# A rotary-embedding kernel: the first small store carries 512 bytes a partition, and batch 0 then leaves whole

## The chip, the cores and the metric

The kernel runs on one core of a Trainium2 chip. The metric is the device time of one execution in microseconds (us); lower is better. The kernel before takes 316.79 us, the median of three runs that lie between 316.6 and 317.02.

## What is computed

Each row of `x` has 64 values, of which the first 32 and the last 32 are rotated against each other by the cosines and sines of their place in the sequence:

```python
def setup_inputs():
    batch, seq_len, num_heads, head_dim = (8, 2048, 16, 64)
    ...
def reference(x, cos, sin):
    x1 = x[..., :head_dim // 2].copy()
    x2 = x[..., head_dim // 2:].copy()
    cos = cos[None, :, None, :].copy()
    sin = sin[None, :, None, :].copy()
    out1 = x1 * cos - x2 * sin
    out2 = x1 * sin + x2 * cos
    return np.concatenate([out1, out2], axis=-1).astype(np.float32)
```

`x` and the result are float32 in HBM, 8 batches of 2048 by 16 by 64. There is little arithmetic for each byte that is moved: each batch is read once and written once.

## The kernel before

**Tiling.** A batch's 2048 sequence positions are spread over the 128 partitions, J = 16 consecutive positions on each. So a partition holds 16 rows of 16 heads by 64 values: 1024 values a row, which are 4 KB in HBM as float32, and 64 KB a partition and batch, contiguous in HBM. In SBUF the rows are float16 (2 KB a row): the DMAs that GpSimd issues convert while they move. The tile `buf` has five slots (NBUF), and batch b uses slot b % 5, so that batches 5, 6 and 7 go into the slots of 0, 1 and 2 once these have been stored.

**The DMAs and their order.** `load` (L71) and `store` (L81) issue on GpSimd's queue. `in_ring` ties each of these DMAs behind the one issued before, so that the order in the program text is the order on the ring. A DMA that must wait for data holds up all that stand behind it on GpSimd. SyncE's queue carries the float32 tables `sin_f` and `cos_f` and the first JA = 2 rows of batch 0 (`head`), and at the end the last two rows of batch 7.

**The arithmetic.** `rotate(b, j0, j1)` is three VectorE instructions on rows j0 to j1 of a batch: the product with the sines with the halves swapped (L92, into `v`), the product with the cosines in place (L98) and the sum in place (L100). ScalarE converts the tables and the head rows (L104 to L110).

**The order around the change.** Load batch 0 (its 14 rows behind the head) and batch 1. When the head rows and the tables are there, rotate rows 0 and 1 of batch 0 and store row 0 (the small first store, L112): it needs L100 of that small rotation, and the loads of batches 2, 3 and 4 (L113, L114) stand behind it. Then rotate the other 14 rows of batch 0 and store rows 1 to 15 (L116), rotate and store batches 1 and 2, load batches 5 and 6 as one DMA when the slots 0 and 1 have been stored, load 7 when slot 2 has been, and so on to the end.

Of the kernel before, what the change touches and what calls it, by code (L numbers as in the profile page):

```python
# [1 line left out]

# [4 lines left out]


@with_exitstack  # L10
def kernel(
    ctx: ExitStack,
    tc: tile.TileContext,
    x: bass.AP,
    cos: bass.AP,
    sin: bass.AP,
    out: bass.AP,
):
    nc = tc.nc
    f16 = mybir.dt.float16  # L20
    f32 = mybir.dt.float32

    B, S, H, D = x.shape
    Dh = D // 2
    P = nc.NUM_PARTITIONS
    J = S // P
    NBUF = 5

    const_pool = ctx.enter_context(tc.tile_pool(name="rope_const", bufs=1))
    io_pool = ctx.enter_context(tc.tile_pool(name="rope_io", bufs=1))  # L30
    tmp_pool = ctx.enter_context(tc.tile_pool(name="rope_tmp", bufs=1))

    JA = 2
    head = const_pool.tile([P, JA, H, D], f32)
    x0 = x[0].rearrange("(p j) h d -> p j (h d)", j=J)
    sin_f = const_pool.tile([P, J, Dh], f32)
    cos_f = const_pool.tile([P, J, Dh], f32)
    cos_h = const_pool.tile([P, J, Dh], f16)
    sin_h = const_pool.tile([P, J, D], f16)
    nc.sync.dma_start(out=sin_f, in_=sin.rearrange("(p j) d -> p j d", j=J))  # L40
    nc.sync.dma_start(  # L41
        out=head.rearrange("p j h d -> p (j h d)"),
        in_=x0[:, 0:JA, :].rearrange("p j f -> p (j f)"),
    )
    nc.sync.dma_start(out=cos_f, in_=cos.rearrange("(p j) d -> p j d", j=J))

    buf = io_pool.tile([P, NBUF, J, H, D], f16)

    ring = []

    def in_ring(dma):
        if ring:
            tc.add_manual_dep(
                dma.ins,
                ring[-1].ins.name,
                mybir.DependencyInfo(mybir.DependencyClass.NoSync, mybir.DependencyReason.DATA),
                reason="order of the ring",
            )
        ring.append(dma)
        return dma  # L60

    def load(b, n=1):
        k = b % NBUF
        if n == 1:
            j0 = JA if b == 0 else 0
            dst = buf[:, k, j0:J, :, :].rearrange("p j h d -> p (j h d)")
            src = x[b].rearrange("(p j) h d -> p j (h d)", j=J)[:, j0:J, :].rearrange("p j f -> p (j f)")
        else:
            dst = buf[:, k : k + n, :, :, :].rearrange("p b j h d -> p b (j h d)")
            src = x[b : b + n].rearrange("b (p j) h d -> p b (j h d)", j=J)  # L70
        in_ring(nc.gpsimd.dma_start(out=dst, in_=src))  # L71

    def store(b, n=1, j0=0, j1=J):
        k = b % NBUF
        if n == 1:
            src = buf[:, k, j0:j1, :, :].rearrange("p j h d -> p (j h d)")
            dst = out[b].rearrange("(p j) h d -> p j (h d)", j=J)[:, j0:j1, :].rearrange("p j f -> p (j f)")
        else:
            src = buf[:, k : k + n, :, :, :].rearrange("p b j h d -> p b (j h d)")
            dst = out[b : b + n].rearrange("b (p j) h d -> p b (j h d)", j=J)  # L80
        return in_ring(nc.gpsimd.dma_start(out=dst, in_=src))  # L81

    def rotate(b, j0=0, j1=J):
        v = tmp_pool.tile([P, J, H, D], f16)
        n = j1 - j0
        js = slice(j0, j1)
        xt = buf[:, b % NBUF, js, :, :]
        shape = [P, n, H, 2, Dh]
        sin_b = sin_h[:, js, :].rearrange("p j (e d) -> p j e d", e=2).unsqueeze(2).to_broadcast(shape)
        cos_b = cos_h[:, js, :].unsqueeze(2).to_broadcast([P, n, 2 * H, Dh])  # L90
        xe = xt.rearrange("p j h (e d) -> p j h e d", e=2)
        nc.vector.tensor_mul(  # L92
            out=v[:, js, :, :].rearrange("p j h (e d) -> p j h e d", e=2),
            in0=xe[:, :, :, ::-1, :],
            in1=sin_b,
        )
        xw = xt.rearrange("p j h (e d) -> p j (h e) d", d=Dh)
        nc.vector.tensor_mul(out=xw, in0=xw, in1=cos_b)  # L98
        xa = xt.rearrange("p j h d -> p (j h d)")
        nc.vector.tensor_add(out=xa, in0=xa, in1=v[:, js, :, :].rearrange("p j h d -> p (j h d)"))  # L100

    load(0)
    load(1)
    nc.scalar.copy(out=sin_h[:, :, Dh:D], in_=sin_f)  # L104
    nc.scalar.mul(out=sin_h[:, :, 0:Dh], in_=sin_f, mul=-1.0)  # L105
    nc.scalar.copy(  # L106
        out=buf[:, 0, 0:JA, :, :].rearrange("p j h d -> p (j h d)"),
        in_=head.rearrange("p j h d -> p (j h d)"),
    )
    nc.scalar.copy(out=cos_h, in_=cos_f)  # L110
    rotate(0, 0, JA)
    store(0, 1, 0, 1)  # L112
    load(2, 2)  # L113
    load(4)  # L114
    rotate(0, JA, J)
    store(0, 1, 1, J)  # L116
    rotate(1)
    store(1)
    rotate(2)
    store(2)  # L120
    load(5, 2)
    load(7)
    rotate(3)
    rotate(4)
    store(3, 2)
    rotate(5)
    rotate(6)
    store(5, 2)
    rotate(7)
    gate = store(7, 1, 0, 9)  # L130
    store(7, 1, 9, J - JA)
    last = buf[:, 7 % NBUF, J - JA : J, :, :].rearrange("p j h d -> p (j h d)")
    dst = out[B - 1].rearrange("(p j) h d -> p j (h d)", j=J)[:, J - JA : J, :].rearrange("p j f -> p (j f)")
    nc.scalar.copy(out=head.rearrange("p j h d -> p (j h d)"), in_=last)  # L134
    end = nc.sync.dma_start(out=dst, in_=head.rearrange("p j h d -> p (j h d)"))
    tc.add_manual_dep(
        end.ins,
        gate.ins.name,
        mybir.DependencyInfo(mybir.DependencyClass.Sync, mybir.DependencyReason.DATA),
        reason="the last rows go out behind this part",  # L140
    )


# [1 line left out]
_INS = ['x', 'cos', 'sin']  # L145
_OUTS = [((8, 2048, 16, 64), 'float32')]


# [23 lines left out]
```

## Time and profile before

| what | value |
|---|---|
| median of three runs | 316.79 us |
| the profiled execution | 316.6 us, of which the span of instructions is 314.8 us |
| DMAs on GpSimd's queue | 14, of which 8 stores |
| the small first store | 512 KB into HBM, 15.2 us from issue to landing |
| batch 0's second store | 7680 KB into HBM, 68.3 us from issue to landing |
| chain that ended last | 66% VectorE, 13% loads that landed late, 8% the load of `cos_f` |

Time from issue to landing contains the time in which a DMA stands behind others on the ring. KB in that list of DMAs are counted at the destination, so that a batch is 4096 KB where it is loaded and 8192 KB where it is stored. In the same way the GB/s of a slice count bytes as they land: the loads show about half of what the stores show, though both move 64 KB of float32 a partition and batch on the side of HBM:

```profile
GB/s 284 187 262 200 200 266 200 200 262 204 200 200 317 382 492 407 400 400 533 400 200 208 258 200 200 229 237 333 400 491 441 400 400 525 408 400 400 433 427 339
```

Stores of batches 0 to 2 are the slices 13 to 20, those of 3 to 7 the slices from 28 on. Packets are counted in the slice or stretch in which they start, with their whole length and time; on all 16 engines they start at nearly the same moment, so a share can exceed 1 in a short stretch and be 0 in the next.

### The profile page before, as it was taken

How to read it: one execution, taken by the hardware profiler on the slowest of the kernel's cores; microseconds unless marked ns; L12 is line 12 of the kernel's file. 1: busy time of each engine (PE TensorE's matmuls, PEld its weight loads, DVE VectorE, ACT ScalarE, POOL GpSimd, SP SyncE). 2: the span in 40 equal slices, each digit the busy share in tenths (PEclk: the TensorE clock that was granted, in tenths of full speed). 3: DMA queues.
4: the chain of work that ended last, by engine and by line, in shares of the span. 5: the costliest groups of instructions: out<-in, count | busy, mean ns of one | idle time of the engine just before them, and what ended most of it. 6: DMA issues, size and time to landing. Idle time of an engine off the chain costs nothing.

```text
span 314.8 us, 115 instructions
## 1 busy us (share of the span) xinstructions
DVE 209.1 (66%) x27; ACT 6.8 (2%) x6; POOL 8.6 (3%) x18
## 2 busy tenths in 40 slices
DVE  0105999999499999999950000899999999910000
ACT  3200000000000000000000000000000000020000
POOL 1002000000000000000010000000000000010000
DMA  9899999999999899999999999999999999999998
GB/s 284 187 262 200 200 266 200 200 262 204 200 200 317 382 492 407 400 400 533 400 200 208 258 200 200 229 237 333 400 491 441 400 400 525 408 400 400 433 427 339
DMA packets 3104, 101.71 MB, mean 323 GB/s; under 512 B 288, under 2 KB 288, under 8 KB 672
## 3 DMA queue, kind: packets, MB, share of 16 engines
q0 software_dynamic: 2528, 99.09, 98.1%
q1 hardware_dynamic: 576, 2.62, 2.2%
HBM read 67.63 MB, written 67.11 MB: 428 GB/s over the span
## 4 chain that ended last, share of the span: by engine, by line
DVE 66%; another core or an unknown queue 13%; DMA 8%; ACT 1%; issue 0%; SPq 0%; DVEq 0%; ACTq 0%
DVE buf L98 22%; DVE buf L100 22%; DVE v L92 22%; DMA cos_f<-in_cos_dram 8%; ACT head L134 1%; ACT cos_h L110 0%; SPq L41 0%; SPq L40 0%; DVEq L92 0%; ACTq L134 0%
## 5 line engine op out<-in xcount | busy, mean ns | idle before, releaser
L92 DVE TENSOR_TENSOR v<-buf,sin_h 128x16384 f16<-128x16384 f16 (+2 forms) x9 | 69.7, 7744 | 51.4 <-DMA buf<-in_x_dram 41.2
L98 DVE TENSOR_TENSOR buf<-buf,cos_h 128x16384 f16<-128x16384 f16 (+2 forms) x9 | 69.7, 7744 | 15.8 <-ACT cos_h L110 15.5
L100 DVE TENSOR_TENSOR buf<-buf,v 128x16384 f16<-128x16384 f16 (+2 forms) x9 | 69.7, 7744 | 0.3
L81 POOL DMA_DIRECT2D out_dram<-buf x8 | 4.7, 586 | 219.4 <-DVE buf L100 219.4
L134 ACT CAST head<-buf 128x2048 f32<-128x2048 f16 x1 | 1.9, 1898 | 249.9 <-DVE buf L100 249.9
L71 POOL DMA_DIRECT2D buf<-in_x_dram x6 | 3.7, 628 | 49.7 <-DMA out_dram<-buf 48.9
L106 ACT CAST buf<-head 128x2048 f16<-128x2048 f32 x1 | 1.9, 1897 | 3.5 <-DMA head<-in_x_dram 3.5
L104 ACT ACT_TABLE_LOAD x1 | 1.3, 1283 | 0.7 <-PEq L156 0.7
L110 ACT CAST cos_h<-cos_f 128x512 f16<-128x512 f32 x1 | 0.6, 617 | 16.1 <-DMA cos_f<-in_cos_dram 16.1
L104 ACT CAST sin_h<-sin_f 128x512 f16<-128x512 f32 x1 | 0.6, 617 | 1.4 <-DMA sin_f<-in_sin_dram 1.4
L105 ACT ACTIVATE sin_h<-sin_f 128x512 f16<-128x512 f32 x1 | 0.6, 624 | 0.0
L156 POOL MEMSET const-float32-0.0<- 128x1 f32 x1 | 0.1, 100 | 0.2 <-issue 0.2
L156 POOL MEMSET const-bfloat16-1.0<- 128x1 bf16 x1 | 0.1, 103 | 0.0
L156 POOL MEMSET const-float32-1.0<- 128x1 f32 x1 | 0.1, 100 | 0.0
L156 POOL MEMSET const-uint8-127<- 128x1 uint8 x1 | 0.1, 100 | 0.0
## 6 DMA issues: line engine op xcount, KB each, us to landing
buf<-in_x_dram POOLq DMA_DIRECT2D x2, 8192.0 KB, 55.2
buf<-in_x_dram POOLq DMA_DIRECT2D x3, 4096.0 KB, 57.4
out_dram<-buf POOLq DMA_DIRECT2D x1, 7680.0 KB, 68.3
out_dram<-buf POOLq DMA_DIRECT2D x1, 4608.0 KB, 28.6
buf<-in_x_dram POOLq DMA_DIRECT2D x1, 3584.0 KB, 22.3
out_dram<-buf POOLq DMA_DIRECT2D x1, 2560.0 KB, 34.1
head<-in_x_dram SPq DMA_DIRECT2D x1, 1024.0 KB, 6.9
out_dram<-head SPq DMA_DIRECT2D x1, 1024.0 KB, 8.4
```

The lines of the kernel that those rows point to most:

```text
L71: in_ring(nc.gpsimd.dma_start(out=dst, in_=src))
L81: return in_ring(nc.gpsimd.dma_start(out=dst, in_=src))
L92: nc.vector.tensor_mul(out=v[:, js, :, :].rearrange("p j h (e d) -> p j h e d", e=2), in0=xe[:, :, :, ::-1, :], in1=sin_b,)
L98: nc.vector.tensor_mul(out=xw, in0=xw, in1=cos_b)
L100: nc.vector.tensor_add(out=xa, in0=xa, in1=v[:, js, :, :].rearrange("p j h d -> p (j h d)"))
L104: nc.scalar.copy(out=sin_h[:, :, Dh:D], in_=sin_f)
L105: nc.scalar.mul(out=sin_h[:, :, 0:Dh], in_=sin_f, mul=-1.0)
L106: nc.scalar.copy(out=buf[:, 0, 0:JA, :, :].rearrange("p j h d -> p (j h d)"), in_=head.rearrange("p j h d -> p (j h d)"),)
L110: nc.scalar.copy(out=cos_h, in_=cos_f)
L134: nc.scalar.copy(out=head.rearrange("p j h d -> p (j h d)"), in_=last)
L156: nc = _bacc.Bacc("TRN2", target_bir_lowering=False, num_devices=1)
```

## The change

The small first store takes the first two heads of row 0 (128 of 1024 values, 512 bytes of the result on each partition, 64 KB in all) in place of the whole row (4 KB, 512 KB in all). It keeps its place in the ring, between the load of batch 1 and that of batches 2 and 3. The later store of batch 0 carries all 16 rows in place of rows 1 to 15, so that the 512 bytes are written twice, with the same values.

```diff
     rotate(0, 0, JA)
-    store(0, 1, 0, 1)
+    in_ring(
+        nc.gpsimd.dma_start(
+            out=out[0].rearrange("(p j) h d -> p j (h d)", j=J)[:, 0, 0:128],
+            in_=buf[:, 0, 0, 0:2, :].rearrange("p h d -> p (h d)"),
+        )
+    )
     load(2, 2)
     load(4)
     rotate(0, JA, J)
-    store(0, 1, 1, J)
+    store(0)
     rotate(1)
     store(1)
```

## The prediction

> **What bounds the kernel now.** I read the page first, its slices, queues and chain, then the order in time, then short stretches.
>
> ```profile
> span 314.8 us, 115 instructions
> DVE 209.1 (66%) x27; ACT 6.8 (2%) x6; POOL 8.6 (3%) x18
> ...
> DMA  9899999999999899999999999999999999999998
> ...
> q0 software_dynamic: 2528, 99.09, 98.1%
> q1 hardware_dynamic: 576, 2.62, 2.2%
> HBM read 67.63 MB, written 67.11 MB: 428 GB/s over the span
> ```
>
> The DMA engines are busy in every slice and the queue that GpSimd feeds fills 98.1% of 16 engines' span. VectorE, though it owns 66% of the chain of waits, idles 41.2 us for loads. So the time is the sum of the packets on the ring, as long as the ring never runs dry. The order in time says whether it does:
>
> ```profile
> 29.53 0.54 POOL L81 DMA_DIRECT2D out_dram<-buf  x1 [27.08 <-DVE buf L100]
> 30.06 1.26 POOL L71 DMA_DIRECT2D buf<-in_x_dram  x2
> ...
> 52.52 0.54 POOL L81 DMA_DIRECT2D out_dram<-buf  x1 [21.19 <-DVE buf L100]
> ...
> 83.38 8.69 DVE L92 TENSOR_TENSOR v<-buf,sin_h 128x16384 f16<-128x16384 f16 x1 [4.99 <-DMA buf<-in_x_dram]
> ...
> 140.72 0.71 POOL L71 DMA_DIRECT2D buf<-in_x_dram  x1 [30.36 <-DMA out_dram<-buf]
> ...
> 250.69 0.73 POOL L81 DMA_DIRECT2D out_dram<-buf  x1 [87.79 <-DVE buf L100]
> ```
>
> At 29.53 the small store goes onto the ring, at 30.06 the loads of batches 2 to 4, while batch 1's load still runs until about 42.7. Batch 0's second part follows at 52.52, long before its turn at 102. The closest issue is that of batches 5 and 6 at 250.69: the ring's work then ends near 256, a margin of 5 us.
>
> Next, what a packet costs. In the software queue a DMA is one packet a partition and batch, and 16 closing ones: ten DMAs of one batch or less and four of two are 10 by 128 + 4 by 256 + 14 by 16 = 2,528, the queue's count above. So one batch is 8 packets on each of 16 engines. In a short stretch, packets = GB/s by length over packet size, and us of one = DMA share by length by 16 over packets.
>
> ```profile
> core 0: us, DVE busy (x) ACT busy (x) POOL busy (x), PEclk, DMA share, GB/s
> 37.40:38.40 1.00, 1.00 (x1) 0.00 (x0) 0.00 (x0) 1.00 2.43 524
> 39.80:40.80 1.00, 1.00 (x1) 0.00 (x0) 0.00 (x0) 1.00 2.83 524
> 42.60:43.90 1.30, 1.30 (x1) 0.00 (x0) 0.00 (x0) 1.00 1.07 366
> 104.00:105.00 1.00, 1.00 (x1) 0.00 (x0) 0.00 (x0) 1.00 2.30 983
> 144.00:145.00 1.00, 0.96 (x2) 0.00 (x0) 0.00 (x0) 1.00 2.45 1049
> 305.70:309.70 4.00, 0.00 (x0) 0.00 (x0) 0.00 (x0) 1.00 1.05 435
> 1.70:2.00 0.30, 0.00 (x0) 0.30 (x1) 0.30 (x2) 1.00 0.77 130
> 3.00:5.00 2.00, 0.00 (x0) 1.15 (x2) 0.00 (x0) 1.00 0.98 415
> ```
>
> First row: 524 GB/s in 1 us is 16 load packets of 32 KB as they land (64 KB as read), 2.43 us each. Third: 366 by 1.3 is 476 KB, 116 packets of the small store's 4 KB, and 1.07 by 1.3 by 16 over 116 is **0.19 us** each. Fourth: 16 packets of batch 0's remaining 60 KB, **2.30**. Fifth: 16 of a whole batch's 64 KB, **2.45**. Sixth: 85 of the 20 KB store near the end, 0.79. These four store sizes lie on one line: (2.45 - 0.19) / 60 is 0.0377 us a KB, and 0.19 - 4 by 0.0377 leaves 0.04 us for a packet of no length. Second row: the last packet of batch 1's load, just ahead of the small store, takes 2.83, so 0.40 more than its fellows. No such excess stands ahead of the whole-batch stores.
>
> **The change part by part**, each term for one engine, since all 16 carry the same.
>
> 1. The 4 KB store goes: 8 by 0.19 = -1.52 us.
> 2. Batch 0's later store carries 64 KB a partition and not 60: 8 by (2.45 - 2.30) = +1.20.
> 3. A store of 512 bytes a partition comes: no row shows such packets. The line gives 0.04 + 0.5 by 0.0377 = 0.06 us, so 8 by 0.06 = +0.48. Bounds: below, the loads on SP's queue in the last row (415 by 2 over 8.192 is 101 packets of 8 KB, 0.31 each, of which 8 by 0.0377 = 0.30 is length) have only 0.01 fixed, so 0.03 each and 0.24 in all, or nothing if the following load's reads cover them; above, a packet that costs no less than the 4 KB one, 0.19 and 1.52 (the seventh row, 2 KB loads at the start, 19 packets, also gives 0.19). I take the line: same queue, same direction, four sizes. Between the ends it is the store row of 4 KB that is nearest, and the line passes through it.
> 4. The 0.40 us ahead of the small store: kept, since what it is seen at is a short store behind a load, and that stays; if it goes with the bytes, -0.40. Nothing in the rows has it grow.
> 5. Hidden: POOL's issue count stays at 14 and the small store's issue stays at 0.54 us, under batch 1's load (13 us of it left at 29.53; without that cover 0.54). Batch 0's whole store now writes bytes of the output that the small one wrote, so it may have to wait for that to land, with the stores of batches 1 and 2 queued behind it on POOL; but the small packets end by 44.4, and the store waits for VectorE until 52.52, 8 us later. The loads of batches 2 and 3 start and land 1.04 us earlier (1.52 - 0.48), which shortens the 4.99 us idle at 83.38; nothing comes of it, since the stores of batches 1 and 2 stand on the ring behind batch 0's. What is late next: batch 1's store lands 0.16 later, the load at 140.72 as well, under batch 2's store (8 by 2.45 = 19.6 us of cover). The 5 us margin at 250.69 loses nothing, since VectorE's chain from there and the ring's shift together.
>
> The sum: -1.52 + 1.20 + 0.48 = **+0.16 us**, 64 KB more over a ring that is always full. The profiled execution took 316.6 (span 314.8 and 1.8 around it), so 316.8; the median of the runs is 316.79, so **316.9** there.
>
> A rule that speaks against the change stands in the Trainium skill: "DMA: Bandwidth & Descriptors", section Bandwidth, lists a GpSimd DMA of 64 KB over 128 partitions (this store's size) at 0.95 us of DMA time and calls transfers below that size dominated by their descriptors. With that for the 0.48 of step 3, an estimate from this page, the sum would be +0.63. The trace of before has no transfer of that size, and the table is of loads.
>
> **The rivals.** A measurement of this kernel can tell about 0.2%, 0.63 us, from no change.
>
> A, the forecast: the packets lie near the line; -0.3 to +0.6 us, about 316.5 to 317.4. For it: four sizes on one line, and the full ring. Chance 0.50.
>
> B, **slower**: a store packet of 512 bytes has a floor, in place of 0.04 of fixed cost, and load(2, 2) starts that much later on all engines. It decides from (0.63 + 0.32) / 8 = 0.12 us a packet on. At 0.19, the price of the 4 KB one, the sum is -1.52 + 1.20 + 1.52 = +1.20, so 318.0. For it: the 2 KB loads at the start at 0.19, and the 0.40 us that shows a short store to cost more than its bytes. Against: the fit's small intercept, and that the start is cold. The 0.95 us of the Trainium skill's "DMA: Bandwidth & Descriptors", section Bandwidth, would be this case at its beginning. Chance 0.33.
>
> C, **faster**: the row's price was mostly one of turning the engines from reads to writes, and a store that small goes under the loads beside it: terms 3 and 4 become 0 and -0.40, -1.52 + 1.20 - 0.40 = -0.72, so 316.1. For it: the excess of 0.40 at this place alone. Against: the engines work their packets one behind the other, and the whole-batch stores behind loads show no excess. It passes 0.2% only where nearly all of both terms goes. Chance 0.14.
>
> D, the change does nothing of the kind, since what counts is only where POOL stands still until 29.53, which stays; then the bytes alone count, 64 KB at 428 GB/s, +0.15 us, so 316.9. Hardly to be told from A. Chance 0.03.
>
> **How the numbers follow.** The likeliest is A: 316.9. The range reaches down to C's 316.1, with 0.1 of scatter (the three runs span 0.4), and up over B's 318.0 by 0.4, for floors above 0.19 that no row bounds: 316.0 to 318.4. Faster by over 0.2%: C's 0.14. Within: A's 0.50 and D's 0.03, 0.53. Slower: B's 0.33. Below 316.0 and above 318.4 I leave about 0.15.
>
> **What would show it.** Right: a short stretch after 42.7 with packets near 0.06 us; a first VectorE instruction of batch 2 at about 82.3 in place of 83.38; batch 0's store with 64 KB packets at 2.45 and 8 of them in 19.6 us; the load behind batch 1's store issued at about 140.9. B shows as that VectorE instruction at or behind 83.3 and the load at 141.9. C: it comes at 81.5, and the load at 140.0. Wrong altogether: a slice of the span with idle DMA engines, a wait on POOL at 52.5 for the small store, or a packet rate away from this line that differs on whole batches.

## The result and the profile after

The changed kernel takes 317.31 us in the median of 15 runs, the kernel before beside it 316.62: a ratio of 1.0027, with a 95% interval of 1.0017 to 1.0037. It is slower by some 0.7 us. The predicted 316.9 is 0.4 too low, within its range of 316.0 to 318.4; a rise of 0.69 lies just above A's bound of +0.6, and the sign is that of rival B, which had 0.33, but not for B's reason. Medians are of all runs, ratios and intervals leave out the few executions, of this and of other kernels here, that took 5 to 9 us longer.

The page and the order in time of the kernel after (columns of the latter as before: start, length, engine, line, operation):

```profile
span 315.5 us, 115 instructions
...
q0 software_dynamic: 2528, 99.16, 98.1%
```
```profile
52.62 0.54 POOL L81 DMA_DIRECT2D out_dram<-buf  x1 [21.19 <-DVE buf L100]
...
81.97 8.69 DVE L92 TENSOR_TENSOR v<-buf,sin_h 128x16384 f16<-128x16384 f16 x1 [3.47 <-DMA buf<-in_x_dram]
...
141.36 0.71 POOL L71 DMA_DIRECT2D buf<-in_x_dram  x1 [32.42 <-DMA out_dram<-buf]
```

The ring is as full as before, and GpSimd waits at 52.62 for VectorE, not for the small store's landing. Batch 2's first VectorE instruction starts at 81.97, 1.41 us earlier than before, where the forecast had 1.04. And yet the load behind batch 1's store is issued at 141.36, 0.64 later than before, where the forecast had 0.16. So what was lost was lost between 82 and 141, after the small store had done better than expected. Short stretches of the kernel after (length, the three engines, the clock, the DMA share, GB/s; with 16 packets in a stretch of 1 us the share is the time of one packet in us):

```profile
39.70:40.70 1.00, 1.00 (x1) 0.00 (x0) 0.00 (x0) 1.00 2.43 524
42.20:43.00 0.80, 0.80 (x1) 0.00 (x0) 0.00 (x0) 1.00 3.67 737
97.90:98.90 1.00, 1.00 (x1) 0.00 (x0) 0.00 (x0) 1.00 3.40 524
214.70:215.70 1.00, 1.00 (x1) 0.00 (x0) 0.00 (x0) 1.00 2.43 524
```

and the last load packets ahead of the two later turns from loads to stores in the kernel before, which the prediction called free of an excess without a row:

```profile
99.40:100.40 1.00, 1.00 (x1) 0.00 (x0) 0.00 (x0) 1.00 2.43 524
214.10:215.10 1.00, 1.00 (x1) 0.00 (x0) 0.00 (x0) 1.00 2.43 524
```

In the second row of the kernel after, 737 by 0.8 is 590 KB: 16 load packets (524 KB) and 128 of 512 bytes (66 KB). Of 3.67 by 0.8 by 16 = 47.0 us, 16 by 2.43 = 38.9 are the loads'; the rest over 128 is 0.063 us a packet, with the closing packets of two DMAs counted in. As recorded, the price of the short packet was met.

A record, however, is longer than the time that its packet takes up on the ring. A stretch inside the small store of the kernel before shows it:

```profile
43.00:43.90 0.90, 0.90 (x1) 0.00 (x0) 0.00 (x0) 1.00 1.26 432
```

432 by 0.9 is 389 KB, 95 packets of 4 KB, so on each engine one starts every 0.152 us, and each is recorded with 1.26 by 0.9 by 16 over 95 = 0.19 us. The 0.04 us between the two is overlap with the next packet, and it is also what the prediction's line gives a packet of no length. So the 4 KB store and the 512-byte one are each about 8 by 0.04 = 0.3 us shorter on the ring than the sum of their records. In the difference of the two this cancels.

But batch 1's last load packet is no longer late (2.43 for 2.83), and the last packet of **batch 4's load, just ahead of batch 0's store**, is: 3.40, an excess of 0.97 us at a place that had none. The first three of the terms that follow come to -1.42, and batch 2's VectorE instruction came 1.41 earlier. The whole sum is -1.52 + 8 by 0.063 - 0.40 + 1.20 + 0.97 = +0.75, against 0.67 between the two profiled executions (317.27 and 316.6).

### The profile page after: what moved, and what is told of

Same layout as the page of the kernel before. It is cut to its first block, busy times and chain, and to the rows that moved or that the text cites. A ratio compares the mean times of both kernels' runs of the same rounds, so it can differ in the third digit from the quotient of the medians.

```text
span 315.5 us, 115 instructions
## 1 busy us (share of the span) xinstructions
DVE 209.1 (66%) x27; ACT 6.8 (2%) x6; POOL 8.6 (3%) x18
## 4 chain that ended last, share of the span: by engine, by line
DVE 66%; another core or an unknown queue 13%; DMA 8%; ACT 1%; issue 0%; SPq 0%; DVEq 0%; ACTq 0%
DVE buf L98 22%; DVE buf L100 22%; DVE v L92 22%; DMA cos_f<-in_cos_dram 8%; ACT head L139 1%; ACT cos_h L110 0%; SPq L41 0%; SPq L40 0%; DVEq L92 0%; ACTq L139 0%
```

## The experiments

What had to be explained is an excess that stands once in an execution: 0.40 us ahead of a row of 4 KB, 0.97 ahead of a whole batch when 512 bytes went first, and none at any later turn (the rows near 99 and 214). **Theory T**: a cost of the first store that is long enough, paid once. **Rival W**: a cost of writing bytes twice. **Rival A**: a cost of addresses written for the first time. Two more theories came out of the runs. **Theory F**: the loads of batches 0 to 4 together last until about 101.55, whatever short store stands among them, and batch 0's store waits for that. **Theory L**: the engines read ahead of what they write, and the excess is the time of a store's first reads, unless the reads are ahead already. In the stretches below, 2.43 is a load packet on time, and each stretch is from one profiled execution of its kernel.

### No small store at all

```diff
-    in_ring(
-        nc.gpsimd.dma_start(
-            out=out[0].rearrange("(p j) h d -> p j (h d)", j=J)[:, 0, 0:128],
-            in_=buf[:, 0, 0, 0:2, :].rearrange("p h d -> p (h d)"),
-        )
-    )
```

> The changed kernel without its first small store; the loads of batches 2 to 4 are therefore issued at about 2.5 us and not at 30. Theory T: the first store of some length in an execution makes the last load packets ahead of it late, once; a row of 4 KB paid 0.40 us, a whole batch of 64 KB packets pays 0.96, 512 bytes pay nothing and spare nothing. Then the last packets of batch 4's load are long by about 0.96 us as in the changed kernel, and the time is 316.62 - 1.51 - 0.40 + 1.20 + 0.96 = 316.9, some 0.46 below the changed kernel. Rival W: the 0.96 came from bytes that are written twice. Here nothing is, so no excess, and 316.62 - 1.51 - 0.40 + 1.20 = 315.9.

317.28 us against 316.63, ratio 1.0021 (1.0011 to 1.003).

```profile
39.70:40.70 1.00, 1.00 (x1) 0.00 (x0) 0.00 (x0) 1.00 2.43 524
81.10:82.10 1.00, 0.01 (x1) 0.00 (x0) 0.00 (x0) 1.00 2.60 524
98.10:99.10 1.00, 1.00 (x1) 0.00 (x0) 0.00 (x0) 1.00 2.96 524
```

Nothing is written twice, and the excess is there, 0.53 ahead of batch 0's store and the rest in smaller pieces from 52 us on (0.17 at 81): W falls. Summed over the records of all its load packets the excess is some 1.1 us, near the 0.96 that T had, but T's time is 0.4 too low: it took the row's removal as 1.51 us, the sum of its records, where 8 by 0.152 = 1.22 leave the ring. The time is that of the changed kernel. On the ring 512 bytes are worth less than their records, and they spare the next turn little (0.97 is left, of some 1.1).

### A row of 4 KB, written twice, and to another place

Both replace the small store of the changed kernel, whose later store of the whole batch stays:

```diff
+    store(0, 1, 0, 1)
```
```diff
+            out=out[1].rearrange("(p j) h d -> p j (h d)", j=J)[:, 0, 0:1024],
+            in_=buf[:, 0, 0, 0:16, :].rearrange("p h d -> p (h d)"),
```

> The small store is the whole row of 4 KB as before, but batch 0 then leaves whole, so the row is written twice. Theory T: excess of about 0.40 us behind batch 1's load, none ahead of batch 0's store; time 316.62 + 1.20 = 317.8. Rival W (bytes written twice): an excess of about 1 us ahead of batch 0's store as well, time 318.8.

> The small store is a row of 4 KB of batch 0's results, but it goes where batch 1's first row belongs, which batch 1's own store overwrites later; batch 0 leaves whole. Theory T: as in the row written twice, 0.40 us behind batch 1's load and none ahead of batch 0's store, 317.8. Rival A: the cost belongs to addresses of the result that were not written before. Then the excess of about 0.96 us is there ahead of batch 0's store, and the time 318.8.

317.91 (ratio 1.0039, 1.0024 to 1.0054) and 317.88 (1.0042, 1.0027 to 1.0057). First the row written twice, then the row in batch 1's place:

```profile
39.60:40.60 1.00, 1.00 (x1) 0.00 (x0) 0.00 (x0) 1.00 2.79 524
99.20:100.20 1.00, 1.00 (x1) 0.00 (x0) 0.00 (x0) 1.00 2.43 524
```
```profile
39.50:40.50 1.00, 1.00 (x1) 0.00 (x0) 0.00 (x0) 1.00 2.80 524
99.10:100.10 1.00, 1.00 (x1) 0.00 (x0) 0.00 (x0) 1.00 2.43 524
```

Both give the 1.2 us of the extra bytes (1.28 and 1.25) and no excess ahead of batch 0's store. A row spares that store its excess even when its bytes go to other addresses: A falls, and W a second time.

### Half a row, a quarter, and one packet on each engine

The small store of the changed kernel with `0:512` and `0:256` in place of `0:128`; and a row of 16 partitions alone:

```diff
+            out=out[0].rearrange("(p j) h d -> p j (h d)", j=J)[0:16, 0, :],
+            in_=buf[0:16, 0, 0, :, :].rearrange("p h d -> p (h d)"),
```

> The small store carries 2 KB a partition (half a row), batch 0 leaves whole. By the line of store packets 8 by 0.115 = 0.92 us, so 316.62 - 1.51 + 0.92 + 1.20 = 317.2 with the 0.40 us of the row. Theory T leaves open from which size on a first store takes the cost on itself: if 2 KB does, the excess is 0.2 to 0.4 us behind batch 1's load and none later, 317.0 to 317.2; if 2 KB does not, the 0.96 us come ahead of batch 0's store, 317.8.

> The small store carries 1 KB a partition, batch 0 leaves whole. Theory F: batch 0's store again starts at 101.5 to 101.6, 317.3. Theory T: 1 KB either pays off the cost (about 0.1 us of excess behind batch 1's load, none later; start near 101.0, 316.7) or spares nothing (0.96 ahead of batch 0's store, start at 101.8, 317.6).

> The small store is the row of 4 KB, but of 16 partitions alone, one packet on each DMA engine in place of eight; batch 0 leaves whole. Theory T (the first store long enough pays once, a packet of 4 KB is): about 0.2 us for the packet and 0.05 to 0.4 of excess behind batch 1's load, none ahead of batch 0's store, so its first packets start near 100.8 and the time is 316.4 to 316.8. Theory F, formed on the runs without a small store and with half a row, where batch 0's store started at 101.52 and 101.58 on the mean of the engines, as in the changed kernel (101.56): the loads of batches 0 to 4 together need until about 101.55, a short store among them runs beside that, and batch 0's store waits for what is left. Then it starts at 101.55, with 0.8 to 1.0 of excess ahead of it, and the time is that of the changed kernel, 317.3.

317.45 (1.0026, 1.0016 to 1.0036), 317.94 (1.0036, 1.0022 to 1.005, of 5 runs; its profiled one took 317.54) and 317.36 (1.0031, 1.0015 to 1.0047). Half a row, a quarter, one packet on each engine:

```profile
39.60:40.60 1.00, 1.00 (x1) 0.00 (x0) 0.00 (x0) 1.00 2.63 524
98.30:99.30 1.00, 1.00 (x1) 0.00 (x0) 0.00 (x0) 1.00 2.80 524
```
```profile
39.70:40.70 1.00, 1.00 (x1) 0.00 (x0) 0.00 (x0) 1.00 2.58 524
98.30:99.30 1.00, 1.00 (x1) 0.00 (x0) 0.00 (x0) 1.00 3.09 524
```
```profile
39.60:40.60 1.00, 1.00 (x1) 0.00 (x0) 0.00 (x0) 1.00 2.43 524
97.70:98.70 1.00, 1.00 (x1) 0.00 (x0) 0.00 (x0) 1.00 3.72 524
```

The cost isn't paid once by whoever comes first: 2 KB pays 0.20 and leaves 0.37 to batch 0's store, 1 KB pays 0.15 and leaves 0.66, one packet of 4 KB an engine pays nothing and leaves 1.29. With 1 KB the load packets before that are late by another 0.3 us in smaller pieces (0.14 at 91). T falls. What is left shrinks as the small store gets longer: its eight packets are recorded with 8 by 0.06 = 0.5 us at 512 bytes (left 0.97), 0.6 at 1 KB (0.66), 0.9 at 2 KB (0.37), 1.5 at 4 KB (0); one packet 0.17 (1.29). Theory F, formed on the first of these and on the kernel without a small store, had the time of the 16 partitions (317.36 for 317.3), though not their excess (1.29 for 0.8 to 1.0), and was too low for the quarter of a row.

### Two rows, and the row behind another load

Both are edits of the kernel before:

```diff
-    store(0, 1, 0, 1)
+    store(0, 1, 0, JA)
...
-    store(0, 1, 1, J)
+    store(0, 1, JA, J)
```
```diff
-    store(0, 1, 0, 1)
     load(2, 2)
+    store(0, 1, 0, 1)
     load(4)
```

> The small store is two rows (8 KB a partition), the later one the other 14; nothing is written twice. Theory F: batch 0's second store would stand on the ring near 103.3, later than 101.55, so no excess ahead of it; what the first row of 4 KB had not to pay is not paid here either, and the time is that of the kernel before, 316.6, up to 0.4 more if the excess behind batch 1's load doubles with the length. Theory T: the excess behind batch 1's load grows towards 0.96 with the length of the first store, 316.8 to 317.2.

> The kernel before, with its small store of one row behind the load of batches 2 and 3 in place of behind batch 1's. Theory T: the first store pays its 0.40 us at about 81, none at 102, and the time is that of before, 316.6. Theory F: the time before batch 0's second store is the same sum, so again 316.6, but the excess at 81 has had 32 packets on each engine to grow and not 16, so 0.6 to 0.8 there, and up to 317.0.

317.29 (1.0012, 0.9994 to 1.0029) and 316.8 (1.0002, 0.9991 to 1.0013). Two rows, then the later row:

```profile
39.60:40.60 1.00, 1.00 (x1) 0.00 (x0) 0.00 (x0) 1.00 3.45 524
101.10:102.10 1.00, 1.00 (x1) 0.00 (x0) 0.00 (x0) 1.00 2.43 524
```
```profile
39.40:40.40 1.00, 1.00 (x1) 0.00 (x0) 0.00 (x0) 1.00 2.43 524
78.30:79.30 1.00, 1.00 (x1) 0.00 (x0) 0.00 (x0) 1.00 3.00 524
99.40:100.40 1.00, 0.97 (x2) 0.00 (x0) 0.00 (x0) 1.00 2.43 524
```

The excess follows the first store wherever it goes, and it grows with that store's length: 1.02 us for two rows, at 40 us, when only batches 0 and 1 have been loaded. F, by which five batches of loads are late together, has no reason for that: it allowed 0.8 at most, and T, which the shorter stores had refuted, forecast the two rows better. The later row pays 0.57, for which T had 0.40 and F 0.6 to 0.8; the times of both kernels can't be told from that of before.

### A row that is read as float32

In place of the row written twice, with the wait for the small rotation kept (`first` is its last instruction):

```diff
+            out=out[0].rearrange("(p j) h d -> p j (h d)", j=J)[:, 0, :],
+            in_=head[:, 0, :, :].rearrange("p h d -> p (h d)"),
...
+    tc.add_manual_dep(
+        early.ins,
+        first.ins.name,
...
```

> As the row written twice, same place, same 4 KB of the result a partition, but taken from the float32 tile head (rows of x that are not rotated; batch 0's store overwrites them). It reads 4 KB a partition and writes 4 KB, where a store from buf reads 2 KB and writes 4. Theory L (lead): the engines read ahead of what they write. At a turn from loads to a store the store's first reads stand in the way of the last load packet, by about 1.0 us where a whole 32 KB packet is read ahead, unless the reads are already ahead; and they get ahead only while a store runs that writes more than it reads, by half to all of its writing time. Then this store gains no lead: excess of 0.8 to 1.1 us behind batch 1's load (it reads 32 KB on each engine, as the two rows did) and 0.6 to 1.1 ahead of batch 0's store, time 318.6 to 319.4. Theory F (batch 0's store only has to start after 101.55) and theory T (a first store of 32 KB on each engine pays once): none ahead of batch 0's store, time 317.9 to 318.5.

318.54 against 316.54, ratio 1.0077 (1.0047 to 1.0106).

```profile
39.60:40.60 1.00, 1.00 (x1) 0.00 (x0) 0.00 (x0) 1.00 3.40 524
99.80:100.80 1.00, 1.00 (x1) 0.00 (x0) 0.00 (x0) 1.00 2.43 524
```

Half of L holds: the same 4 KB of the result cost 0.97 us of excess when 4 KB are read for them and 0.36 to 0.40 when 2 KB are. So the excess seems to go by what the store **reads**: 32 KB on an engine here as in the two rows (0.97 and 1.02), 16 KB in the row of float16. One thing more differs: this store converts nothing, where the others turn float16 into float32, and no run separates the two. The other half of L fell: none is left ahead of batch 0's store, though this store writes no more than it reads. L was mended: what spares the next turn is the time for which the store writes, whatever it reads.

### The turn at another place

The kernel without a small store, with batch 0's store ahead of batch 4's load:

```diff
     load(2, 2)
-    load(4)
     rotate(0, JA, J)
     store(0)
+    load(4)
```

> The changed kernel without its small store, and with batch 0's store ahead of the load of batch 4 on the ring, so that the first turn from loads to a store comes behind 32 load packets on each engine and not 40. Theory L, mended after the float32 row: the excess at a turn is the time of the store's first reads (about 1.0 us for 32 KB on an engine), less the writing time of the stores that ran before; so 0.8 to 1.1 us at the first turn, now near 80, and none at the turn from batch 4's load to batch 1's store near 122. The end is that of the kernel without a small store, 317.3. Theory F: what is late are the five batches of loads together, by 101.55; at 80 nothing is late yet, or 0.8 us if it grows with the packets, and some may come at the second turn.

317.44 against 316.63, ratio 1.003 (1.0014 to 1.0046).

```profile
78.30:79.30 1.00, 0.33 (x1) 0.00 (x0) 0.38 (x1) 1.00 3.43 524
118.20:119.20 1.00, 1.00 (x1) 0.00 (x0) 0.00 (x0) 1.00 2.43 524
```

1.00 us at the first turn, which now comes at 79, none at the second, behind batch 4's load. The mended L had both and the time. F had nothing at 80, or 0.8, and with the two rows against it as well it falls.

### Without the second writing, and the row in two halves

The first is an edit of the changed kernel:

```diff
-    store(0)
+    in_ring(
+        nc.gpsimd.dma_start(
+            out=out[0].rearrange("(p j) h d -> p (j h d)", j=J)[:, 128:],
+            in_=buf[:, 0, :, :, :].rearrange("p j h d -> p (j h d)")[:, 128:],
+        )
+    )
```

> The changed kernel, but batch 0's later store leaves out the 512 bytes that have gone, so that nothing is written twice; it still has one packet a partition, of 63.5 KB. All theories but W: 8 by 0.5 KB by 0.0377 = 0.15 us less than the changed kernel, 317.15, with the same excess of about 0.96 us ahead of that store. W (the excess comes of bytes that are written twice): 316.2.

317.14 against 316.54, ratio 1.0019 (1.001 to 1.0028).

```profile
97.80:98.80 1.00, 1.00 (x1) 0.00 (x0) 0.00 (x0) 1.00 3.24 524
```

It takes 0.60 us more than the kernel before, where the changed kernel takes 0.69 more, and 0.81 of excess stands ahead of batch 0's store. Writing 512 bytes twice was never the matter.

The second is an edit of the kernel before:

```diff
-    store(0, 1, 0, 1)
+    in_ring(
+        nc.gpsimd.dma_start(
+            out=out[0].rearrange("(p j) h d -> p (j h d)", j=J)[:, 0:512],
+            in_=buf[:, 0, :, :, :].rearrange("p j h d -> p (j h d)")[:, 0:512],
+        )
+    )
     load(2, 2)
+    in_ring(
+        nc.gpsimd.dma_start(
+            out=out[0].rearrange("(p j) h d -> p (j h d)", j=J)[:, 512:1024],
+            in_=buf[:, 0, :, :, :].rearrange("p j h d -> p (j h d)")[:, 512:1024],
+        )
+    )
     load(4)
```

> The kernel before, with its row of 4 KB in two halves of 2 KB, the first behind batch 1's load, the second behind the load of batches 2 and 3; nothing is written twice. Theory L: 0.19 us of excess at 42 as with half a row, then 0.65 us of lead, so none at 81, then again lead, so none ahead of batch 0's store: 0.2 us less than before, 316.4 to 316.6. Theory T: 0.19 at 42, and the rest of the cost later, 0.2 or more at 81: 316.6 or more. Theory F: the natural start of batch 0's second store is 101.8 to 102.0, behind 101.55, so no excess ahead of it.

316.25 against 316.54, ratio 0.9993 (0.9984 to 1.0002).

```profile
39.70:40.70 1.00, 1.00 (x1) 0.00 (x0) 0.00 (x0) 1.00 2.45 524
79.10:80.10 1.00, 0.00 (x0) 0.00 (x0) 0.07 (x1) 1.00 2.43 524
99.10:100.10 1.00, 0.97 (x2) 0.00 (x0) 0.00 (x0) 1.00 2.43 524
```

All three turns are on time, 0.38 us of excess less than before at the first of them. L had forecast none at the second and the third, but 0.19 at the first, where 0.02 stands. The median is 0.3 us below that of before, but the interval still takes in no change; the stretches are the better evidence that the excess is gone.

## Why the prediction was right and wrong

**Right.** What bounds the kernel: the ring stayed full, and every gain and loss came out of packets. The term for the four KB more of batch 0 holds, the record of the short packet is as forecast (0.063 for 0.06), and B's floor of 0.12 or more is not there. The two terms of the small stores, -1.52 and +0.48, are sums of records and each about 0.3 us too large for the ring, since the 0.04 us of a packet of no length is overlap; it is luck that the one is taken off and the other added. The wait on GpSimd that the double writing might have brought does not show at 52.62. The Trainium skill, "DMA: Bandwidth & Descriptors", section Bandwidth, would have had 0.95 us for a transfer of this size: here the 64 KB take 8 by 0.063 = 0.5 us by their records on each engine, as a store in the middle of a full ring, where the page's table is of loads, so the measurement decides for the lower figure.

**Wrong: step 4**, the excess of 0.40 us "ahead of the small store: kept". It was seen at one turn only and taken for a property of a short store behind a load; that the whole-batch stores showed none was taken for a property of theirs. The runs show that it belongs to the first turn from loads to stores, grows with the store that stands there, and is spared later by what has been written before. So it did not stay: -0.40 at 42 us and +0.97 at 98. Without this step's error the sum would have been +0.75; with it, +0.16. That 316.9 lies only 0.4 off is in part luck: the 0.40 that went makes up for part of the 0.97 that came, and the range was wide for other reasons, B's floor and C. Rival C had seen that the 0.40 may go and was right in that, and had nothing come in its place; its objection, that the whole-batch stores behind loads show no excess, was the same error. D, that only the standing still of GpSimd counts, falls too: without a small store GpSimd doesn't stand still there, and the time is the changed kernel's.

**The cause, as far as it is shown.** Shown: the place of the excess (the runs with the first store moved, shortened, lengthened or left out); that it grows at the first turn with the length of the store there (0.15 us where that reads 4 KB on an engine, 0.02 and 0.20 for 8, 0.36 to 0.57 for 16, about 1.0 for 32); and that a store recorded with 1.3 us or more before spares the next turn all of it, with 0.9 us most, with 0.6 us some. That it goes by the bytes read and not by those written rests on the float32 row alone. Argued: that the engines read ahead of what they write, so that a store's first 32 KB are fetched while the last load packet is still under way and delay it; and that, while a store writes, the reads of the loads behind it run on and are ahead from then on. No row shows the reads by themselves. Open: the excess ahead of equal stores differs between executions of one profile each (0.36 to 0.57 for a row, 0.02 and 0.20 for half a row, 0.81 and 0.97 behind 512 bytes). The same 4 KB on an engine leave 0.97 as eight packets and 1.29 as one. And in the kernel without a small store about half of the 1.1 came in small pieces from 52 us on, when batch 0's store was already on the ring.

## What to carry to other kernels

On a ring that is always full, a small transfer between two large ones can be worth more than its bytes: compare the last packet ahead of every turn from loads to stores, and ask which earlier one spared it. When a trace shows a cost at one of several like places, it may be one that moves and not one that goes with the place. Here a store of a row between the loads is about the right size: shorter, and the next turn pays 0.4 to 1.3 us; longer, and its own turn pays 1.0. Do not add up packet records as if they stood one behind the other: where they overlap, the sum is too large.

## What the runs showed of the hardware that was not expected

A turn from loads to stores costs up to 1.3 us on all 16 engines at once, and a later turn costs nothing once a store has been written for long enough (3.43 us for a packet of 2.43 at 79, and 2.43 at the next turn). The packet that shows it is the load's, not the store's. It seems to go by the bytes at the source: a row in float32 cost 0.97, the same row in float16 0.36 to 0.40. And a store packet's recorded time is a straight line from 512 bytes (0.063 us) to 64 KB (2.45), with about 0.04 us at no length, and those 0.04 overlap the next packet: packets of 4 KB are recorded with 0.19 us and start 0.152 apart.
